# Reordering the output product of a hybrid RWKV-7 / short-convolution layer on one core

## The chip, the cores and the metric

The kernel runs on one core of one Trainium2 chip. The metric is the device time of one execution in microseconds (us), of which a smaller number is better. Every time in this part is from the runs of the kernel before or from the trace of one profiled execution of it.

## The reference

One layer takes 512 tokens, with 16 learned tokens put before them, each 2048 wide.

```python
hn = rmsnorm(h_res, norm_in_g)
P = hn @ w_in                              # 2048 -> 65 column groups of 128
r, k, v, g_r, wl, al = token_shift(P[:, :4224])    # RWKV-7 branch, 16 heads x 64
Bg, Cg, hc, g_c = split(P[:, 4224:])               # convolution branch, 1024 wide
y_a = (group_norm(recurrence(r, decay, k, v, kk, kk * a)) + bonus) * silu(g_r)
y_b = Bg * causal_conv3(Cg * hc, conv_w) * silu(g_c)
mix = concat([y_a, y_b])                   # 2048 wide
h_res = h_res + mix @ w_out                # 2048 x 2048
out = rmsnorm(h_res, norm_f_g)[16:]
```

All values are float32.

## The kernel before

**Stages.** The input projection (`mains`, `steps`) makes 65 column groups of 128 with TensorE. The RWKV branch is worked out beside it in four rounds of two head pairs: `prepare` makes the operands of one pair, `invert` inverts the triangular systems of two pairs, and `recur` then runs the recurrence over nine chunks. When the projection's last group (`ps_gc`) is done, the output product follows, with the final RMS norm at its end. On TensorE the order is the program's own. The other engines' instructions, SyncE's DMA queue among them, are put in order by a scheduler, except for the last stretch of the kernel, whose order is written out by hand.

**Precision.** Every large matmul is done three times, as high x high, high x low and low x high parts. The high part of a tensor is a copy that ScalarE rounds (CAST), the low part is a subtraction on VectorE of two operands (TENSOR_TENSOR). A "split" below is this pair of instructions.

**The work between matmuls.** `fill(ns)` puts that much projection work (in the program's own estimate) into TensorE's order, so that another engine has time for the next step of `prepare`, `invert` or `recur`. The table `FW` holds the amounts. In `invert`, `fill(FW["solve_first"])` stands ahead of the first use of the inverse: VectorE's transposes `xn` (L844) and then TensorE's `t` (L853).

**The output product.** `mix @ w_out` is done for two halves of 1024 output columns. In each half the operands are cut into 2 x 2 quarters and multiplied by seven products in place of eight (a Strassen-Winograd scheme): `M1`, `M2`, `P5`, `M7`, `M3`, `Q6`, `P4`. The left operands are parts of `mix` (for M1, M2, P4) or four sums of such parts, the forms `S1`, `S3`, `S4`, `S5`, each made for two quarters of mix rows, q = 0 and 1 (`sums` on VectorE, then `split_form`; tiles named `S` in the trace). The right operands are blocks of `w_out` (128 x 1024), or sums of such blocks.

A product of one half is cut in four parts g = 0 to 3 along the inner dimension. One `(half, product, g)` is a **unit**, called a block here: twelve matmuls of 512 columns. The list `units` is the order of the 56 blocks on TensorE. In the kernel before it is, for each half, M1 (4 blocks), then for each g the four blocks P5, M7, M3, Q6, then P4 and M2: mixed with each other in the first half, P4 ahead of M2 in the second. The half-1 M2 blocks are not in that loop: they end the kernel (`end`, `ends`).

**Weights of a block.** Three kinds of buffers are used.

- `raw` is a ring of three buffers, which the projection's weights (`wr`) use before and `request` uses here (tiles `wo`).
- `chain` is one tile per g (`x` in the trace). `begin_chain` loads it on SyncE's queue, `add_by_transfer` adds another block to it by an accumulating DMA on GpSimd's queue, `add` adds one on VectorE (L1204). P5, Q6 and P4, and M1 with another content, take their weights from it. In half 0 the tiles 0 to 2 are loaded while the projection still runs; tile 3 lies in a pool (`pw`) that opens when the projection's buffers are given up.
- The split parts go to a ring of six slots (`w` of the projection, `o` here), two for a block, so a block's slots come free when the block three places ahead is done. The half-1 M2 weights are split early into buffers of their own (`load_home`).

`at(u, fn, ...)` puts a step in front of block u. After the four blocks of a product, `close` adds its result to the output tiles `xa` (columns 0 to 1023) or `xb` (1024 to 2047) on VectorE (`onto`, L1222) and takes squares on ScalarE. `gain` multiplies finished tiles by the norm's weights `gfb`; eight of these run on GpSimd (L1299). At the end `row_scale` makes the RMS factor of a token tile, with a power on GpSimd (`rsqrt`, L98), and `finish` and `finish_last` scale the output and store it.

```python
    for half in range(2):
        units += [(half, "M1", g) for g in range(4)]
        units += [(half, prod, g) for g in range(4) for prod in ("P5", "M7", "M3", "Q6")]
        ends = ("P4", 0), ("P4", 1), ("M2", 0), ("P4", 2), ("M2", 1), ("P4", 3), ("M2", 2), ("M2", 3)
        units += [(half, prod, g) for prod, g in sorted(ends, key=lambda e: half and e[0] == "M2")]
```

Of the kernel before, what the change touches and what calls it, by code (L numbers as in the profile page):

```python
# [9 lines left out]
F32 = mybir.dt.float32  # L10
# [3 lines left out]
ALU = mybir.AluOpType  # L14
# [4 lines left out]
P = 128  # L19
# [58 lines left out]
def hymba_kernel(ctx: ExitStack, tc: tile.TileContext, xt, xtok, front, w_in, w_out, pv, lup, cst, msk, gf, out):  # L78
    nc = tc.nc
# [3 lines left out]
    wp = ctx.enter_context(tc.tile_pool(name="wp", bufs=3))  # L83
# [105 lines left out]
    raw = {}  # L189
# [920 lines left out]
    def quarter(k, tk, q):  # L1110
        return mix[2 * k + q][:, :, tk]

    def sums(q):
        a11, a21, a12, a22 = quarter(0, T0, q), quarter(0, T1, q), quarter(1, T0, q), quarter(1, T1, q)
        nc.vector.tensor_tensor(out=a22, in0=a22, in1=a21, op=ALU.subtract)
        nc.vector.tensor_tensor(out=a21, in0=a11, in1=a21, op=ALU.subtract)
        nc.vector.scalar_tensor_tensor(out=a11, in0=a22, scalar=-1.0, in1=a11, op0=ALU.mult, op1=ALU.subtract)
        nc.vector.scalar_tensor_tensor(out=a12, in0=a11, scalar=-1.0, in1=a12, op0=ALU.mult, op1=ALU.subtract)

    for j in range(NPAIR, NPAIR + 4):  # L1120
        split_mix(j)
# [13 lines left out]
    for j in range(NPAIR + 4, KT):  # L1135
        while ("gc", j - NPAIR) not in ready:
            step()
        run_pending(float("inf"))
        split_mix(j)
    for _ in flow:  # L1140
        pass
    prefetch(len(stream))
    ph1.close()


# [16 lines left out]


    LEFT = {"M1": 0, "M2": T0, "M7": "S3", "Q6": "S5", "P5": "S1", "P4": T1, "M3": "S4"}
    units = []
    for half in range(2):
        units += [(half, "M1", g) for g in range(4)]
        units += [(half, prod, g) for g in range(4) for prod in ("P5", "M7", "M3", "Q6")]
        ends = ("P4", 0), ("P4", 1), ("M2", 0), ("P4", 2), ("M2", 1), ("P4", 3), ("M2", 2), ("M2", 3)
        units += [(half, prod, g) for prod, g in sorted(ends, key=lambda e: half and e[0] == "M2")]  # L1170
    U = {unit: u for u, unit in enumerate(units)}
    right, straight = {}, {}

    def left(prod, jj, part, s):
        w = LEFT[prod]
# [4 lines left out]
            return parts[jj][part][:, tk]  # L1180
        return parts[NPAIR + jj][part][:, w][:, tk]

    def rows_of(half, k, col, g):
        return w_out[2 * half + col, 4 * k + g]

    def begin_chain(half, g):
        if half or g == 3:
            chain[g] = new_chain(half, g)  # L1190
        nc.sync.dma_start(chain[g], rows_of(half, 0, 0, g))

    def request(half, k, col, g):
        t = wp.tile([P, 1024], F32, tag="raw", name=f"wo{half}{k}{col}{g}", bufs=3)
        state["dma"] = nc.sync.dma_start(t, rows_of(half, k, col, g)).ins
        straight[half, k, col, g] = t
# [83 lines left out]
    def at(u, fn, *args):  # L1280
        calls.setdefault(max(u, -1), []).append((fn, args))
# [31 lines left out]
    def passing(*block):  # L1313
        return lambda: straight[block]

    def chained(g):
        return lambda: chain[g]

    for half in range(2):
        o = 28 * half  # L1320
        for g in range(4):
            b = o + 4 + 4 * g
            if half == 0:
                if g == 3:
                    at(-1, begin_chain, 0, g)
                    at(0, split_unit, (0, "M1", g), chained(g))
            else:
                at(o + g - 4, begin_chain, 1, g)
                at(o + g - 2, split_unit, (1, "M1", g), chained(g))
            at(max(o + g, b - 5), add_by_transfer, half, 0, 1, g)  # L1330
# [10 lines left out]
            if half == 0:  # L1341
# [79 lines left out]
    with tc.manual_schedule(engines={mybir.EngineType.DVE, mybir.EngineType.Activation, mybir.EngineType.Pool}):  # L1421
        end = po.tile([P, 512], F32, tag="o", name="end")
        for g in range(4):
            product((1, "M2", g), [end], (0,))
        for t in (2, 3):
            row_part(t, 3)
            row_scale(t, 3)
        row_part(0, 3)
        row_part(1, 3)
        finish(2, (2, 0, 3))  # L1430
        finish(3, (2,))
        nc.vector.tensor_tensor(out=here(0, 2), in0=here(0, 2), in1=end, op=ALU.add)
        squares(0, 2)
        row_scale(0, 3)
        finish(3, (0, 3))
        gain(1, 3, nc.vector)
        ends = [po.tile([P, 256], F32, tag="o", name=f"end{part}") for part in range(2)]
        for part in range(2):
            cols = slice(256 * part, 256 * part + 256)
            for jj in range(8):  # L1440
                hi, lo = right[(1, "M2", jj // 2), jj % 2]
                for n, (m, w) in enumerate(((0, hi), (0, lo), (1, hi))):
                    nc.tensor.matmul(
                        ends[part], left("M2", jj, m, 1), w[:, cols], start=(jj == 0 and n == 0), stop=(jj == 7 and n == 2)
                    )
            h = here(1, 2)[:, cols]
            nc.vector.tensor_tensor(out=h, in0=h, in1=ends[part], op=ALU.add)
# [70 lines left out]
```

## Time and profile before

| what | value |
|---|---|
| median of 3 runs | 1012.8 us (1012.61 to 1014.0) |
| time of the profiled execution | 1012.36 us |
| its span, first to last instruction | 1010.6 us |
| TensorE (PE) busy | 995.3 us, 98% |
| VectorE (DVE) busy | 684.2 us, 68% |
| ScalarE (ACT) busy | 393.8 us, 39% |
| GpSimd (POOL) busy | 276.8 us, 27% |
| granted TensorE clock, mean | 0.998 |
| last matmul of the projection, first of the output product | 842.09 us, 842.31 us |

Times in the trace count from the start of the span. A row of the timeline has the start, the length, the engine, the line, the operation, the tiles (output <- inputs), the shape and how many like instructions follow each other; in brackets stands how long the engine was idle before the row, and what ended that. The ends of matmuls are modelled and matmuls overlap, so a wait of TensorE is read best from the starts of rows: with no wait a block of twelve matmuls takes a fixed time.

### The profile page before, as it was taken

Reading aid. Unit: us, or ns where it says so; the run is one execution under the profiler, and the core shown is the slowest. Engines: PE = TensorE matmul, PEld = TensorE weight load, DVE = VectorE, ACT = ScalarE, POOL = GpSimd, SP = SyncE. Lnnn points to the kernel's source line nnn. Section 1 sums busy time; section 2 is a strip of 40 time slices with the busy share of each in tenths; the row PEclk is TensorE's granted clock in tenths of the full one; section 3 lists DMA queues with packets and bytes.
Section 4 is the critical chain, followed back from the end, with each engine's and each line's share of the span. In section 5 each row is a group of like instructions: output and inputs, shape, how many; then the busy total and the mean of one; then the engine's idle time right before and its main releaser. Section 6 shows DMA issues by size and latency. Waiting matters only on the chain.

```text
span 1010.6 us, 23763 instructions
## 1 busy us (share of the span) xinstructions
PE 995.3 (98%) x9723; PEld 913.0 (90%) x9723; DVE 684.2 (68%) x1305; ACT 393.8 (39%) x729; POOL 276.8 (27%) x294
## 2 busy tenths in 40 slices
PE   9999999999999999999999999999999999999996
PEld 8999998999998999998999998889898897787875
DVE  7686955588765668654668653254555697998787
ACT  7553423344323434322434322222222335445453
POOL 0123314233232423232324222222333332015001
PEclk9999999999999999999999999999999999999999
DMA  9526476346764363854273856977772798695654
GB/s 331 156 73 151 121 203 171 108 124 152 173 162 145 93 170 98 221 148 120 84 187 92 211 140 207 339 244 228 217 213 76 212 262 192 168 325 140 173 122 167
DMA packets 185037, 174.83 MB, mean 173 GB/s; under 512 B 121568, under 2 KB 142816, under 8 KB 184416
## 3 DMA queue, kind: packets, MB, share of 16 engines
q1 hardware_dynamic: 182336, 164.40, 56.5%
q0 software_dynamic: 2304, 8.39, 5.0%
q8 instruction: 76, 1.25, 0.5%
q10 hardware_dynamic: 288, 0.52, 0.1%
q14 instruction: 33, 0.27, 0.1%
HBM read 136.92 MB, written 36.35 MB: 171 GB/s over the span
## 4 chain that ended last, share of the span: by engine, by line
PE 56%; DVE 8%; DMA 3%; issue 2%; ACT 1%; POOL 0%; DVEq 0%; ACTq 0%; SPq 0%; POOLq 0%
PE ps_gc L328 8%; PE ps_B L328 7%; PE ps_h L328 7%; PE ps_C L328 7%; PE ps_k L328 5%; PE ps_v L328 5%; PE ps_g L328 5%; PE ps_r L328 5%; DVE o L1214 3%; DMA wo<-in_w_out_dram 2%; PE M L1241 2%; PE zy L1010 1%; PE zs L1006 1%; PE g L681 1%; DVE xb L1222 1%
## 5 line engine op out<-in xcount | busy, mean ns | idle before, releaser
L135 POOL TENSOR_TENSOR w<-wr,w 128x512 fp32r<-128x512 f32 x119 | 167.5, 1408 | 358.2 <-ACT w L134 307.4
L134 ACT CAST w<-wr 128x512 fp32r<-128x512 f32 x252 | 153.2, 618 | 286.4 <-PE ps_k L328 46.8
L135 DVE TENSOR_TENSOR w<-wr,w 128x512 fp32r<-128x512 f32 x133 | 96.1, 729 | 102.2 <-ACT w L134 102.0
L328 PE MATMUL ps_r<-xh,w 128*128 128x256 f32 (+1 forms) x512 | 95.5, 282 | 0.0
L328 PE MATMUL ps_k<-xh,w 128*128 128x256 f32 (+1 forms) x512 | 95.5, 284 | 0.0
L328 PE MATMUL ps_v<-xh,w 128*128 128x272 f32 (+1 forms) x512 | 95.1, 283 | 0.0
L328 PE MATMUL ps_h<-xh,w 128*128 128x258 f32 (+1 forms) x512 | 94.0, 282 | 0.7 <-issue 0.7
L328 PE MATMUL ps_C<-xh,w 128*128 128x258 f32 (+1 forms) x512 | 93.2, 281 | 0.0
L328 PE MATMUL ps_g<-xh,w 128*128 128x258 f32 (+1 forms) x512 | 92.2, 281 | 0.0
L328 PE MATMUL ps_B<-xh,w 128*128 128x512 f32 x256 | 83.6, 395 | 0.1
L328 PE MATMUL ps_gc<-xh,w 128*128 128x512 f32 x256 | 81.5, 393 | 0.2 <-DVE w L135 0.2
L328 PEld LDWEIGHTS ps_h<-xh,w 128*128 128x128 f32 x512 | 79.7, 189 | 1.5 <-issue 0.8
L328 PEld LDWEIGHTS ps_k<-xh,w 128*128 128x128 f32 x512 | 80.4, 189 | 0.2
L328 PEld LDWEIGHTS ps_r<-xh,w 128*128 128x128 f32 x512 | 80.4, 189 | 0.2
L328 PEld LDWEIGHTS ps_v<-xh,w 128*128 128x128 f32 x512 | 80.1, 189 | 0.3
L328 PEld LDWEIGHTS ps_C<-xh,w 128*128 128x128 f32 x512 | 79.7, 189 | 0.6
L328 PEld LDWEIGHTS ps_g<-xh,w 128*128 128x128 f32 x512 | 79.4, 189 | 0.5
L328 PE MATMUL ps_k<-xl,w 128*128 128x272 f32 (+1 forms) x256 | 73.0, 285 | 0.0
L328 PE MATMUL ps_v<-xl,w 128*128 128x256 f32 (+1 forms) x256 | 72.5, 283 | 0.0
L328 PE MATMUL ps_r<-xl,w 128*128 128x256 f32 (+1 forms) x256 | 72.3, 282 | 0.0
L328 PE MATMUL ps_g<-xl,w 128*128 128x256 f32 (+1 forms) x256 | 72.2, 282 | 0.0
L328 PE MATMUL ps_C<-xl,w 128*128 128x256 f32 (+1 forms) x256 | 71.9, 281 | 0.0
(321 smaller groups left out, 2275.6 us busy)
## 6 DMA issues: line engine op xcount, KB each, us to landing
wr<-in_w_in_dram SPq DMA_DIRECT2D x126, 512.0 KB
ct<-opd SPq DMA_DIRECT2D x64, 288.0 KB
wo<-in_w_out_dram SPq DMA_DIRECT2D x24, 512.0 KB
x<-in_w_out_dram POOLq DMA_DIRECT2D x16, 512.0 KB, 5.8
opd<-ar SPq DMA_DIRECT2D x8, 576.0 KB
opd<-gt SPq DMA_DIRECT2D x16, 288.0 KB
opd<-bt SPq DMA_DIRECT2D x64, 64.0 KB
x<-in_w_out_dram SPq DMA_DIRECT2D x8, 512.0 KB
```

Of the source, the lines that this page charges most:

```text
L134: nc.scalar.copy(hi, rq)
L135: low[q] = eng.tensor_tensor(out=lo, in0=rq, in1=hi.bitcast(F32), op=ALU.subtract).ins
L328: nc.tensor.matmul(ps[r], ww[:, w], xx[:, kt, a:b], start=(kt == 0 and n == 0), stop=(kt == KT - 1 and n == 2))
L681: nc.tensor.matmul(z[h][:, c - c0], bk[hs, c, h : h + 2, :].rearrange("p a s -> p (a s)"), ar[hs, c].rearrange("p a s -> p (a s)"), start= ...
L1006: nc.tensor.matmul(d[hs, j], w, x[hs], start=(a == 0), stop=(a == b - 1))
L1010: nc.tensor.matmul(d[ho, j], t[hs, o : o + CH], x[hs], start=(a == 0), stop=(a == b - 1))
L1214: nc.vector.tensor_tensor(out=lo, in0=rq, in1=hi.bitcast(F32), op=ALU.subtract)
L1222: nc.vector.tensor_tensor(out=h, in0=h, in1=ps, op=op)
L1241: nc.tensor.matmul(bank[s], left(prod, jj, m, s), w, start=(jj == 0 and n == 0), stop=(jj == 7 and n == 2))
```

## The change

- **Order of the blocks.** In half 0 the four M2 blocks stand right behind the four M1 blocks and ahead of the first P5. The P4 blocks of half 0 end that half, and the first M1 block of half 1 stands ahead of the last P4 block. Half 1 keeps its order. The steps that load and split weights move with their blocks.
- **Weights of the fourth M1 block of half 0** come through a `raw` buffer, requested while the projection still runs, instead of through chain tile 3. That tile is loaded later, at block 2.
- **Forms.** The four sums of `sums(1)` are spread over blocks 6 to 9, and the eight `split_form` steps over blocks 1 to 14.
- **First inverse.** `FW["solve_first"]` gets 1100 more, so more projection work stands ahead of the first inverse's matmuls.
- **End.** The last `gain` of the token tile 1 (256 columns, VectorE) stands behind `row_scale` instead of ahead of it, and one `finish` of token tile 0 behind the last addition instead of ahead of it.

```diff
-        fill(FW["solve"] + 2400 * (first == 2) if first else FW["solve_first"])
+        fill(FW["solve"] + 2400 * (first == 2) if first else FW["solve_first"] + 1100)
...
     prefetch(len(stream))
+    straight = {}
+    request(0, 0, 0, 3)
     ph1.close()
...
+    def block(half):
+        return [(half, prod, g) for g in range(4) for prod in ("P5", "M7", "M3", "Q6")]
+
+    units = [(0, prod, g) for prod in ("M1", "M2") for g in range(4)] + block(0)
+    units += [(0, "P4", 0), (0, "P4", 1), (0, "P4", 2), (1, "M1", 0), (0, "P4", 3)]
+    units += [(1, "M1", g) for g in range(1, 4)] + block(1) + [(1, prod, g) for prod in ("P4", "M2") for g in range(4)]
...
+    at(0, split_unit, (0, "M1", 3), passing(0, 0, 0, 3))
+    at(2, begin_chain, 0, 3)
...
-            if half == 0:
-                at(U[half, "M2", g] - 4, request, 0, 1, 0, g)
-                at(U[half, "M2", g] - 2, split_unit, (0, "M2", g), passing(0, 1, 0, g))
+            if half:
+                at(m2 + 2 * g - g - 11, load_home, g)
             else:
-                at(o + 13 + 2 * g, load_home, g)
+                at(m2 - 5, request, 0, 1, 0, g)
+                at(m2 - 2, split_unit, (0, "M2", g), passing(0, 1, 0, g))
     for n, f in enumerate(("S1", "S3", "S4", "S5")):
-        at(n, split_form, f, 0)
-        if n == 2:
-            at(n + 1, sums, 1)
-        at(6 + n, split_form, f, 1)
+        at((1, 2, 4, 5)[n], split_form, f, 0)
+        at(6 + n, sums, 1, (n,))
+        at((10, 11, 13, 14)[n], split_form, f, 1)
...
-            gain(1, 2, nc.vector, cols)
             if part == 0:
-                finish(0, (2, 0, 3))
+                gain(1, 2, nc.vector, cols)
+                finish(0, (2, 0))
                 nc.vector.tensor_tensor(out=fv[:, 1, 0:1], in0=fv[:, 1, 0:1], in1=ssq[:, 1, 3:4], op=ALU.add)
+        finish(0, (3,))
         row_scale(1, 4, nc.vector)
+        gain(1, 2, nc.vector, slice(256, 512))
         finish_last(1)
```

Three places of the engines' orders are shown, as the built programs have them, before and after. A row has the line, the operation, output <- inputs with buffer numbers, and the shape.

VectorE, from the last projection split of `mix` on, before (`x_11314` is chain tile 3, `x_11136` chain tile 0, `wo` raw buffers, `o` slots, `S` forms):

```order
L1105 TENSOR_TENSOR m_11274<-mix_10660,m_11273 128x512
L1115 TENSOR_TENSOR mix_10660<-mix_10660,mix_10658 128x4x256
L1161 TENSOR_TENSOR S_11295<-mix_10659,S_11294 128x1024
L1161 TENSOR_TENSOR S_11291<-mix_10657,S_11290 128x1024
L1214 TENSOR_TENSOR o_0_11317<-x_11314,o_0_11317 128x512
L1214 TENSOR_TENSOR o_1_11320<-x_11314,o_1_11320 128x512
L1214 TENSOR_TENSOR o_0_11355<-x_11136,o_0_11355 128x512
L1214 TENSOR_TENSOR o_1_11358<-x_11136,o_1_11358 128x512
L1161 TENSOR_TENSOR S_11297<-mix_10659,S_11296 128x1024
L1214 TENSOR_TENSOR o_0_11378<-wo_11310,o_0_11378 128x512
```

The same place after (the splits' line is L1216, the forms' L1174):

```order
L1105 TENSOR_TENSOR m_11274<-mix_10660,m_11273 128x512
L1216 TENSOR_TENSOR o_0_11314<-wo_11277,o_0_11314 128x512
L1216 TENSOR_TENSOR o_1_11317<-wo_11277,o_1_11317 128x512
L1118 TENSOR_TENSOR mix_10660<-mix_10660,mix_10658 128x4x256
L1174 TENSOR_TENSOR S_11297<-mix_10659,S_11296 128x1024
L1216 TENSOR_TENSOR o_0_11356<-wo_11312,o_0_11356 128x512
L1216 TENSOR_TENSOR o_1_11359<-wo_11312,o_1_11359 128x512
L1174 TENSOR_TENSOR S_11293<-mix_10657,S_11292 128x1024
L1174 TENSOR_TENSOR S_11299<-mix_10659,S_11298 128x1024
L1216 TENSOR_TENSOR o_0_11383<-wo_11320,o_0_11383 128x512
```

The fourth M1 block's split (the first two `o` rows of each) is now first and reads a raw buffer, and M2 splits (`wo_11312`, `wo_11320`) stand where those of P5 and M7 stood.

GpSimd, from the chain additions of the end of half 0 on, before (DMA rows are chain additions, the others are gains):

```order
L1200 DMA x_11138<-in_w_out_dram 128x1024
L1200 DMA x_11314<-in_w_out_dram 128x1024
L1299 TENSOR_TENSOR xa_11308<-xa_11308,gfb 128x512
L1299 TENSOR_TENSOR xa_11306<-xa_11306,gfb 128x512
L1299 TENSOR_TENSOR xa_11309<-xa_11309,gfb 128x512
L1299 TENSOR_TENSOR xa_11307<-xa_11307,gfb 128x512
L1299 TENSOR_TENSOR xa_11308<-xa_11308,gfb 128x512
L1200 DMA x_11860<-in_w_out_dram 128x1024
L1299 TENSOR_TENSOR xa_11309<-xa_11309,gfb 128x512
L1200 DMA x_11880<-in_w_out_dram 128x1024
```

The same place after:

```order
L1301 TENSOR_TENSOR xa_11308<-xa_11308,gfb 128x512
L1301 TENSOR_TENSOR xa_11309<-xa_11309,gfb 128x512
L1202 DMA x_11138<-in_w_out_dram 128x1024
L1202 DMA x_11354<-in_w_out_dram 128x1024
L1202 DMA x_11826<-in_w_out_dram 128x1024
L1301 TENSOR_TENSOR xa_11310<-xa_11310,gfb 128x512
L1301 TENSOR_TENSOR xa_11308<-xa_11308,gfb 128x512
L1301 TENSOR_TENSOR xa_11311<-xa_11311,gfb 128x512
L1202 DMA x_11872<-in_w_out_dram 128x1024
L1301 TENSOR_TENSOR xa_11309<-xa_11309,gfb 128x512
```

Two gains moved ahead of the chain additions for P4's last blocks (`x_11138`, `x_11354`), and the first chain addition of half 1 (`x_11826`) moved ahead of the other six gains. The first of those six needs the result of P4.

VectorE at the very end, before (`end` is the result of the last products, L1393 and L1299 are `row_scale` and `gain`):

```order
L1403 SCALAR_TENSOR_TENSOR xb_11802<-xb_11802,fv,gfb 128x512
L1452 TENSOR_TENSOR fv<-fv,ssq 128x1
L1447 TENSOR_TENSOR xb_11780<-xb_11780,end_12546 128x256
L1299 TENSOR_TENSOR xb_11780<-xb_11780,gfb 128x256
L1393 TENSOR_SCALAR fv<-ssq,fv 128x1
```

The same place after:

```order
L1450 TENSOR_TENSOR fv<-fv,ssq 128x1
L1445 TENSOR_TENSOR xb_11781<-xb_11781,end_12548 128x256
L1401 SCALAR_TENSOR_TENSOR xb_11806<-xb_11806,fv,gfb 128x512
L1391 TENSOR_SCALAR fv<-ssq,fv 128x1
L1301 TENSOR_TENSOR xb_11781<-xb_11781,gfb 128x256
```

The finish (L1401) moved behind the last addition, and the gain (L1301) behind `row_scale` (L1391).

More of the change, by code (lines that the diff above doesn't have):

```diff
@@ L1111, in quarter, with sums @@
         return mix[2 * k + q][:, :, tk]
-    def sums(q):
+    def sums(q, which=range(4)):
         a11, a21, a12, a22 = quarter(0, T0, q), quarter(0, T1, q), quarter(1, T0, q), quarter(1, T1, q)
[L1115 to L1118, printed above, removed]
+        for n in which:
+            if n < 2:
+                o, x = ((a22, a22), (a21, a11))[n]
+                nc.vector.tensor_tensor(out=o, in0=x, in1=a21, op=ALU.subtract)
+            else:
+                o, x = ((a11, a22), (a12, a11))[n - 2]
+                nc.vector.scalar_tensor_tensor(out=o, in0=x, scalar=-1.0, in1=o, op0=ALU.mult, op1=ALU.subtract)
     for j in range(NPAIR, NPAIR + 4):
@@ L1139, in hymba_kernel, with rows_of, request @@
         split_mix(j)
+    def rows_of(half, k, col, g):
+        return w_out[2 * half + col, 4 * k + g]
+    def request(half, k, col, g):
+        t = wp.tile([P, 1024], F32, tag="raw", name=f"wo{half}{k}{col}{g}", bufs=3)
+        state["dma"] = nc.sync.dma_start(t, rows_of(half, k, col, g)).ins
+        straight[half, k, col, g] = t
     for _ in flow:
@@ L1164, in hymba_kernel @@
     LEFT = {"M1": 0, "M2": T0, "M7": "S3", "Q6": "S5", "P5": "S1", "P4": T1, "M3": "S4"}
[L1165 to L1170, printed above, removed]
+    def block(half):
[3 more added lines that the diff above has]
+    units += [(1, "M1", g) for g in range(1, 4)] + block(1) + [(1, prod, g) for prod in ("P4", "M2") for g in range(4)]
     U = {unit: u for u, unit in enumerate(units)}
-    right, straight = {}, {}
+    right = {}
     def left(prod, jj, part, s):
@@ L1191, in begin_chain @@
         nc.sync.dma_start(chain[g], rows_of(half, 0, 0, g))
[L1193 to L1196, printed above, removed]
     def add_by_transfer(half, k, col, g):
@@ L1317, in chained @@
         return lambda: chain[g]
+    at(0, split_unit, (0, "M1", 3), passing(0, 0, 0, 3))
+    at(2, begin_chain, 0, 3)
     for half in range(2):
-        o = 28 * half
         for g in range(4):
-            b = o + 4 + 4 * g
-            if half == 0:
[L1324 to L1330, printed above, removed]
+            b, m1, m2 = U[half, "P5", g], U[half, "M1", g], U[half, "M2", g]
+            if half:
+                at(m1 - 4, begin_chain, 1, g)
+                at(m1 - 2, split_unit, (1, "M1", g), chained(g))
+            at(max(m1 + (half == 0 and g == 3), b - 5), add_by_transfer, half, 0, 1, g)
             at(b - (6 if g else 5), request, half, 0, 1, g)
```

4 lines of the change are left out of this document (1 added, 3 removed).

## Prediction

> **What bounds the kernel now.** I read the page first, then TensorE's timeline over the output product, then VectorE, ScalarE and GpSimd over the same stretch, and last the projection as one window.
>
> ```profile
> span 1010.6 us, 23763 instructions
> PE 995.3 (98%) x9723; PEld 913.0 (90%) x9723; DVE 684.2 (68%) x1305; ACT 393.8 (39%) x729; POOL 276.8 (27%) x294
> 178.00:842.30 664.30, 663.52 (x7576) 620.50 (x7569) 413.99 (x829) 223.91 (x414) 206.15 (x198) 1.00 0.62 171
> ```
>
> TensorE is busy for 98% of the span, and the change removes no matmul. What can be won is time in which TensorE stands, and the row of the window (length, then busy time of PE, PEld, DVE, ACT and POOL) says that between the first inverse and the end of the projection it stands for 0.8 us of 664. So the output product is what to look at:
>
> ```profile
> 842.31 8.33 PE L1241 MATMUL M<-w,m 128*128 128x512 f32 x36
> 851.52 0.51 PE L1241 MATMUL M<-o,m 128*128 128x512 f32 x1 [0.88 <-ACT o L1213]
> 854.90 2.89 PE L1241 MATMUL P<-o,S 128*128 128x512 f32 x12
> 862.14 2.14 PE L1241 MATMUL M<-o,S 128*128 128x512 f32 x8 [0.71 <-DVE o L1214]
> 865.07 2.80 PE L1241 MATMUL Q<-o,S 128*128 128x512 f32 x11 [0.57 <-DVE o L1214]
> 878.95 2.88 PE L1241 MATMUL P<-o,S 128*128 128x512 f32 x12
> 917.02 9.55 PE L1241 MATMUL M<-o,m 128*128 128x512 f32 x40
> 926.81 3.01 PE L1241 MATMUL M<-o,m 128*128 128x512 f32 x12 [0.24 <-DVE o L1214]
> 930.16 4.84 PE L1241 MATMUL M<-o,m 128*128 128x512 f32 x20 [0.34 <-DVE o L1214]
> 934.85 2.88 PE L1241 MATMUL P<-o,S 128*128 128x512 f32 x12
> 970.21 5.94 PE L1241 MATMUL M<-o,S 128*128 128x512 f32 x24
> 990.71 0.61 PE L1241 MATMUL end<-home,m 128*128 128x512 f32 x2
> ```
>
> Fourteen blocks lie between 878.95 and 917.02, with no wait in them: 38.07 us, 2.719 us a block. By this measure TensorE loses 12.59 - 4 x 2.719 = 1.71 us from 842.31 to 854.90, 24.05 - 8 x 2.719 = 2.30 us up to 878.95, 17.83 - 6 x 2.719 = 1.52 us from 917.02 to 934.85, nothing over the 13 blocks after that, and 20.50 - 7 x 2.719 = 1.47 us from 970.21 to 990.71. Together 7.0 us: all that a better order of blocks can give.
>
> **Why it waits.** Four rows for the first two losses:
>
> ```profile
> 845.46 0.33 SPq L1191 DMA_DIRECT2D x<-in_w_out_dram  x1
> 850.85 2.18 ACT L1213 CAST o<-x 128x512 fp32r<-128x512 f32 x4 [1.95 <-DMA x<-in_w_out_dram]
> 864.34 2.49 DVE L1214 TENSOR_TENSOR o<-x,o 128x512 fp32r<-128x512 f32 x4
> 855.00:875.00 20.00, 20.00 (x26) 1.00 0.59 139
> ```
>
> The fourth M1 block's weights are asked for at 845.46, when the projection's buffers come free, and land at about 850.8, after the block could have begun (842.31 + 3 x 2.719 = 850.47). Then VectorE is busy for 20.00 of 20.00 us: eight forms, four sums and the weights of P5 to Q6 all fall due within it. A split takes 0.60 us there (four in 2.49, with a tail of 0.08), a 1024-wide sum or form 1.14. For the third loss:
>
> ```profile
> 902.76 1.28 DVE L1266 TENSOR_TENSOR sh<-sh,Q 128x512 f32<-128x512 f32 x2
> 907.61 4.69 DVE L1222 TENSOR_TENSOR xa<-xa,sh 128x512 f32<-128x512 f32 x4
> 909.75 1.39 POOL L1299 TENSOR_TENSOR xa<-xa,gfb 128x512 f32<-128x512 f32 x1 [0.30 <-ACT sqj_None L1228]
> 925.38 1.38 DVE L1214 TENSOR_TENSOR o<-x,o 128x512 fp32r<-128x512 f32 x1 [0.76 <-ACT o L1213]
> 928.72 5.17 DVE L1214 TENSOR_TENSOR o<-x,o 128x512 fp32r<-128x512 f32 x5 [0.16 <-ACT o L1213]
> 842.50:936.30 93.80, 87.50 (x113) 1.00 0.75 208
> ```
>
> Two VectorE instructions take 1.28 us beside no GpSimd work; four with both operands in SBUF take 4.69 us beside GpSimd's gains, and single splits 1.38. So a gain costs VectorE up to 1.1 us. TensorE's waits at 926.81 and 930.16 end just behind such splits.
>
> **The change, part by part.** *M2 behind M1, the fourth M1 block from a raw buffer.* The raw buffer's request stands ahead of the chains in SyncE's queue, during the projection, so its weights lie ready; the 1.71 us go. M2 needs no form and no sum, only splits, so P5 of g = 0 begins at block 8, not 4: 842.31 + 8 x 2.719 = 864.06 where nothing waits. I counted VectorE's new order against this, from 846.8 (the end of the last split of `mix`, which stays) at 0.60 and 1.14 us a row. The second M7 split of g = 1 is done at 877.2, against 842.31 + 13 x 2.719 + 0.68 = 878.3, the tightest place of this part; P5 of g = 0 at 862.0 against 864.7. The raw ring's requests pass too: M2's third weights are asked for when M1's fourth are split (848.0), and even 5.4 us (asked 845.46, cast 850.85) leave them over 4 us ahead of block 6. So I take all of the 2.30 us too.
>
> *P4 late, M1 of half 1 among it.* Chain tile 0 of half 1 is asked for behind P4's first split and is due at block 27 (915.7); VectorE's count brings both there early. What decides is VectorE's total. From 842.5 to the end of M7's first split in half 1 (936.3) it was busy 87.5 of 93.8 us, 6.3 idle. In the new order the same stretch holds one 1024-wide addition more, which earlier ran under the projection: 88.6 us. That split is due at 842.31 + 33 x 2.719 + 0.68 = 932.7, which leaves it 1.6 us of idling in place of 6.3. Since a block's slots come free only three blocks later, it can't run far ahead and will stand when it has caught up, by my count some 3 us around blocks 20 to 23. That makes it about 1.4 us late. The two ends: 0 if it idles under 1.6 us, 4.7 if it idles as much as before. I take 1.4, since VectorE's count has it two to three us ahead of most blocks, which is work done in time that was idle. GpSimd's six gains behind P4 fall into just these blocks, where they were spread over 907 to 933 before. So of 1.71 + 2.30 + 1.52 = 5.53 us I expect 4.1.
>
> *The end of half 1.* The order there is the same but for buffers, and VectorE's lead on TensorE about the same: 0, between 0.45 gained (VectorE half a us earlier in its chain of weight requests) and 1.0 lost.
>
> *First inverse.*
>
> ```profile
> 170.04 2.37 DVE L135 TENSOR_TENSOR w<-wr,w 128x512 fp32r<-128x512 f32 x2
> 172.34 0.70 DVE L844 STREAM_TRANSPOSE xn<-xT 128x512 f32<-128x512 f32 x1
> 173.09 0.69 PE L853 MATMUL t<-xn,gt 64*64 64x64 f32 x32 [0.79 <-DVE xn L844]
> ```
>
> Ten projection matmuls of 272 columns, 10 x 0.12 = 1.2 us by the same pace, now stand ahead of these. The 0.79 us go, and the transpose does not move on VectorE. I take 0.8 off.
>
> *The end of the kernel.*
>
> ```profile
> 996.14 5.91 PE L1443 MATMUL end<-home,m 128*128 128x256 f32 x48
> 1001.24 1.41 DVE L1403 SCALAR_TENSOR_TENSOR xb<-xb,fv,gfb 128x512 f32<-128x512 f32 x2
> 1002.63 0.41 DVE L1447 TENSOR_TENSOR xb<-xb,end 128x256 f32<-128x256 f32 x1
> 1003.68 0.42 DVE L1299 TENSOR_TENSOR xb<-xb,gfb 128x256 f32<-128x256 f32 x1 [0.64 <-ACT sqj L1228]
> 1004.02 0.21 DVE L1393 TENSOR_SCALAR fv<-ssq,fv 128x1 f32<-128x1 f32 x1
> 1004.31 0.55 POOL L98 TENSOR_TENSOR fv<-fv,mhalf 128x1 f32<-128x1 f32 x1 [3.62 <-DVE fv L1393]
> 995.89 0.30 POOL L1393 TENSOR_SCALAR fv<-ssq,fv 128x1 f32<-128x1 f32 x1
> 999.52 0.52 POOL L1393 TENSOR_SCALAR fv<-ssq,fv 128x1 f32<-128x1 f32 x1 [2.40 <-ACT sqj_None L1228]
> ```
>
> TensorE is done at 1002.05; the last addition (1002.63) waits for two finishes on VectorE. With one moved behind it, it starts about 0.5 us sooner, and the finish runs under ScalarE's squares. With the gain moved behind `row_scale`, that row comes a further 0.34 us sooner (1004.02 - 1003.68): 0.8 together. But the gain then runs beside GpSimd's power. A GpSimd row of the same form took 0.30 us alone and 0.52 beside a gain, so I give 0.3 of it back and take 0.5 (0.3 to 0.8). The Trainium skill (SBUF — State Buffer, "SBUF: two separate sides") says that VectorE with two SBUF inputs and GpSimd share one port pair that is locked for a whole instruction. By that the power waits for the rest of the gain; the trace's 1.38 us splits agree, and this term is then 0.5, without the lock 0.8.
>
> **The sum.** 4.1 + 0 + 0.8 + 0.5 = 5.4 us off the profiled execution's 1012.36, which is 0.44 under the median: 1007.0, or **1007.4** on the median's scale. The likely case's own range is 1006.0 to 1009.4.
>
> **Rivals.**
>
> *All waits go.* VectorE idles little, and its gains meet idle time: 5.53 + 0.45 + 0.8 + 0.8 = 7.6 us off, 1005.2. For it speaks that one of the gains before (at 919.60) fell into VectorE's idle time; against it, that 88.6 of 90.2 us must then be work. Chance 0.20.
>
> *VectorE is what sets the pace.* It idles as much as before, since slots and chains hold it, and the end of half 1 starts late: 4.7 us come back there and 1.0 at the end. 5.53 - 4.7 - 1.0 + 0.8 + 0.3 = 0.9 us off, 1011.9, no measurable change. For it: 20.00 busy of 20.00. Against: VectorE has M2's 10.9 us more before the forms fall due. Chance 0.13, of which 0.08 end within 0.2%.
>
> *Slower: the weights of the low-rank step come late in the projection.* The later inverse re-lays VectorE's order for some 40 us. The split `lul` of the next head pair moves from ahead of `te` to behind the transpose `vs`:
>
> ```profile
> 203.71 0.96 DVE L595 TENSOR_TENSOR lul<-lur,luh 128x256 fp32r<-128x256 f32 x1 [0.47 <-ACT luh L594]
> 216.55 0.78 DVE L821 STREAM_TRANSPOSE vs<-v 128x576 f32<-128x576 f32 x1
> 230.14 0.29 PE L572 MATMUL tz<-la,lul 128*128 128x272 f32 x1
> ```
>
> It would be done at about 218, 12 us ahead of its matmul. Held up for longer than that, TensorE, in its fixed order, stands for every us beyond, and it has no slack in the projection. 20 us of delay cost 8: 1012.36 + 8 - 5.4 = 1015.0, 1015.4 on the median's scale. It is slower from 12 + 5.4 us on. Against it: 12 us of lead. Chance 0.07.
>
> The forecast keeps 0.60. The range takes in all the first rival and most of the second: 1004.4 to 1011.0. Faster by over 0.2% (2.0 us, about what a measurement here can tell from no change): 0.60 + 0.20 + 0.05 = 0.85; within it 0.08; slower 0.07.
>
> **What would show it.** Right: the first P block starts 22 us behind the first output matmul, with no wait of TensorE in the eight blocks ahead; no wait at L853 near 173; the first P block of half 1 starts 88 to 89 us behind the first output matmul (92.5 before), with gains on GpSimd and VectorE rows of 1.3 us and more right there. The sum is wrong if TensorE waits anew between 175 and 842, if M2's blocks wait for a DMA, or if the first P block of half 1 starts under 87.3 us or over 91 us behind the first.

## The result, and the profile after

| | kernel before | changed kernel |
|---|---|---|
| median of 11 runs of each | 1013.52 us (1012.36 to 1014.97) | 1010.73 us (1008.48 to 1013.13) |
| ratio of the two, 95% interval | 1 | 0.9973 [0.9964, 0.9983] |
| profiled execution | 1012.36 us | 1008.48 us |

The changed kernel is 2.7 us faster (0.27%), where 5.4 us were forecast. Both profiled executions are the fastest of their eleven, and the changed kernel's times spread over 4.7 us where those of the kernel before spread over 2.6. So one trace does not tell all of this result, and the experiments below give twelve more traces.

The page of the changed kernel, first lines of the part on engines:

```profile
span 1006.6 us, 23759 instructions
PE 993.2 (99%) x9723; PEld 912.7 (91%) x9723; DVE 683.2 (68%) x1305; ACT 393.0 (39%) x729; POOL 288.0 (29%) x294
```

TensorE's timeline over the output product, with the places that answer to those shown of before:

```profile
842.02 8.33 PE L1243 MATMUL M<-w,m 128*128 128x512 f32 x36
850.19 13.76 PE L1243 MATMUL M<-o,m 128*128 128x512 f32 x60
863.79 2.88 PE L1243 MATMUL P<-o,S 128*128 128x512 f32 x12
907.31 8.32 PE L1243 MATMUL P<-o,m 128*128 128x512 f32 x36
929.07 2.92 PE L1243 MATMUL P<-o,S 128*128 128x512 f32 x12
931.83 0.39 PE L1243 MATMUL M<-o,S 128*128 128x512 f32 x1
933.16 5.55 PE L1243 MATMUL M<-o,S 128*128 128x512 f32 x23 [0.95 <-DVE o L1216]
939.28 2.77 PE L1243 MATMUL Q<-o,S 128*128 128x512 f32 x11 [0.35 <-DVE o L1216]
969.67 2.82 PE L1243 MATMUL M<-o,S 128*128 128x512 f32 x11 [0.19 <-DVE o L1216]
981.68 5.51 PE L1243 MATMUL P<-o,m 128*128 128x512 f32 x23 [0.28 <-DVE o L1216]
987.03 5.15 PE L1243 MATMUL end<-home,m 128*128 128x512 f32 x22
```

The first P block starts 863.79 - 842.02 = 21.77 us behind the first output matmul, just what eight blocks take, and TensorE does not wait until 931.83. The waits at the start of the output product are gone. From 931.83 on it waits for VectorE's splits: in the second and the fourth block behind the M1 blocks of half 1 (numbers 33 and 35, counted from 0), and again near the end. The 52 blocks take 987.03 - 842.02 = 145.01 us, of which 145.01 - 52 x 2.719 = 3.6 us are waits (7.0 before).

What VectorE and GpSimd do just ahead of that first wait (rows of each engine in turn):

```profile
914.28 7.21 POOL L1301 TENSOR_TENSOR xa<-xa,gfb 128x512 f32<-128x512 f32 x1 [1.02 <-ACT sqj_None L1230]
925.47 1.59 POOL L1301 TENSOR_TENSOR xa<-xa,gfb 128x512 f32<-128x512 f32 x1
927.32 1.90 POOL L1301 TENSOR_TENSOR xa<-xa,gfb 128x512 f32<-128x512 f32 x1
929.18 2.23 POOL L1301 TENSOR_TENSOR xa<-xa,gfb 128x512 f32<-128x512 f32 x1
914.30 2.50 DVE L1224 TENSOR_TENSOR xa<-xa,sh 128x512 f32<-128x512 f32 x4
917.91 1.22 DVE L1206 TENSOR_TENSOR wo<-wo,wo 128x1024 f32<-128x1024 f32 x1
919.05 1.29 DVE L1216 TENSOR_TENSOR o<-x,o 128x512 fp32r<-128x512 f32 x2
920.25 0.69 DVE L1224 TENSOR_TENSOR xa<-xa,P 128x512 f32<-128x512 f32 x1
925.38 4.45 DVE L1216 TENSOR_TENSOR o<-x,o 128x512 fp32r<-128x512 f32 x1
929.86 2.64 DVE L1206 TENSOR_TENSOR x<-x,wo 128x1024 f32<-128x1024 f32 x1
```

A gain begins at 914.28 and lasts 7.21 us, while VectorE runs one instruction with two SBUF operands behind the other; it ends just behind the first VectorE row with a PSUM operand (920.25). Then it is GpSimd that keeps VectorE out: one split (two take 1.29 us at 919.05) lasts 4.45 us and ends only behind two gains and the two chain additions issued among them, and the 1024-wide addition behind it takes 2.64 us in place of 1.22. TensorE's wait at 931.83 is for the splits that stand behind these two rows.

### The profile page after: what moved, and what is told of

Same layout as the page of the kernel before. It is cut to its first block, busy times and chain, and to the rows that moved or that the text cites. A ratio compares the mean times of both kernels' runs of the same rounds, so it can differ in the third digit from the quotient of the medians.

```text
span 1006.6 us, 23759 instructions
## 1 busy us (share of the span) xinstructions
PE 993.2 (99%) x9723; PEld 912.7 (91%) x9723; DVE 683.2 (68%) x1305; ACT 393.0 (39%) x729; POOL 288.0 (29%) x294
## 4 chain that ended last, share of the span: by engine, by line
PE 62%; DVE 5%; DMA 2%; issue 2%; ACT 0%; POOL 0%; DVEq 0%; ACTq 0%; POOLq 0%
PE ps_gc L328 8%; PE ps_B L328 7%; PE ps_h L328 7%; PE ps_C L328 7%; PE ps_k L328 5%; PE ps_v L328 5%; PE M L1243 5%; PE ps_g L328 5%; PE ps_r L328 5%; DVE o L1216 2%; PE P L1243 2%; DMA wo<-in_w_out_dram 2%; PE Q L1243 1%; PE zy L1010 1%; PE zs L1006 1%
```

## The experiments

A table of all traces first. Kernels of one group of runs share the runs of the kernel before, so ratios compare better than medians. "Start" is the first output matmul. The next four columns are what TensorE loses in the output product against 2.719 us a block, worked out from the starts of its rows: in blocks 0 to 7, 8 to 26, 27 to 35 and 36 to 51. "End" is the time from the end of block 51 to the end of the span. All in us.

| kernel | median (runs) | ratio to before, 95% | start | 0-7 | 8-26 | 27-35 | 36-51 | end |
|---|---|---|---|---|---|---|---|---|
| before | 1013.5 (11) | 1 | 842.31 | 3.64 | 0.38 | 1.51 | 1.48 | 19.89 |
| changed | 1010.73 (11) | 0.9973 [0.9964, 0.9983] | 842.02 | 0.02 | 0.02 | 1.95 | 1.63 | 19.53 |
| a1, changed again | 1009.36 (5) | 0.9965 [0.9952, 0.9977] | 842.39 | 0.02 | 0.02 | 1.36 | 2.75 | 19.43 |
| a2, changed again | 1008.24 (1) | - | 842.13 | 0.02 | 0.02 | 1.42 | 1.95 | 19.40 |
| no_gain | 1006.36 (5) | 0.9924 [0.9911, 0.9938] | 842.53 | 0.02 | 0.02 | 0.01 | 0.54 | 19.47 |
| g_dve2 | 1007.74 (5) | 0.9943 [0.9930, 0.9955] | 842.76 | 0.02 | 0.02 | 0.01 | 2.04 | 19.59 |
| g_dve3 | 1005.76 (5) | 0.9926 [0.9913, 0.9939] | 842.38 | 0.02 | 1.47 | 0.01 | 0.49 | 19.17 |
| g_dve4 | 1005.51 (5) | 0.9920 [0.9907, 0.9934] | 841.82 | 0.02 | 0.02 | 0.01 | 0.15 | 19.19 |
| g_pool2 | 1009.17 (5) | 0.9961 [0.9947, 0.9975] | 842.08 | 0.02 | 0.02 | 1.45 | 2.46 | 19.45 |
| c3late | 1009.19 (5) | 0.9954 [0.9941, 0.9966] | 842.29 | 0.02 | 0.02 | 1.37 | 2.41 | 19.61 |
| no_inv | 1010.16 (5) | 0.9967 [0.9954, 0.9979] | 843.08 | 0.02 | 1.28 | 2.48 | 2.12 | 19.21 |
| tail0 | 1010.51 (7) | 0.9976 [0.9965, 0.9987] | 842.26 | 0.02 | 0.88 | 2.43 | 1.90 | 19.83 |
| b_ng, old order | 1011.24 (11) | 0.9978 [0.9969, 0.9987] | 843.88 | 4.37 | 0.37 | 0.01 | 0.02 | 19.80 |
| raw, old order | 1011.92 (11) | 0.9990 [0.9981, 0.9999] | 843.40 | 2.27 | 0.38 | 1.27 | 1.37 | 19.88 |

**The changed kernel again (a1, and later a2).**

> The changed kernel as it is, for a second trace and for the spread of its times (1008.5 to 1013.1 so far, where the kernel before had 1012.4 to 1015.0). Theory P (a GpSimd gain and a VectorE instruction with two SBUF inputs shut each other out, so that the start of half 1 depends on how they fall): a time in the middle of the spread goes with TensorE waits of 2 to 5 us at blocks 27 to 36, where the first trace shows 1.8 us, and the rest of the trace agrees within 0.5 us. Rival Q (the spread comes from waits that the change does not touch, such as those of the projection near 760 and at the kernel's start): the blocks 27 to 36 lose 1.8 us again, and the difference of the spans lies ahead of 842.

> The changed kernel as it is, for a third trace. Five traces have the same output product and the same GpSimd gains (the changed kernel twice, without the later inverse, with the old end, and with VectorE gains as a contrast). If its time is set by two things that fall differently each time, the landing of M2's last weights near 857 (VectorE waited 0.5 us for it in one trace, 2.3 and 2.5 in others) and how the gains and VectorE meet from 915 on, then the time from the first output matmul to the end of P4 of half 1 lies between 145.0 and 147.3 us, and the share over 141.4 (52 blocks of 2.719) splits into a part in blocks 8 to 27 of the size of VectorE's wait near 857 less 1 us, and the rest behind block 27.

Both theories of a1 were partly right. The losses behind block 26 are 3.6, 4.1 and 3.4 us in the three traces of the same program; in a1 and a2 the first of the late gains got through in 1.77 us, and the waits fell in blocks 30 and 31 instead of 33 and 35. The starts differ by 0.4 us as well. Neither trace is from the slow end of the spread (1012 to 1013), so what such an execution loses was not seen. From the first output matmul to the end of P4 of half 1 a2 takes 144.8 us, just under the 145.0 to 147.3 that were expected. The split of its expectation holds: VectorE does not wait near 857, nothing is lost in blocks 8 to 26, and the rest lies behind.

**Without six gains (no_gain), and with them on VectorE (g_dve2).**

```diff
-    for n in range(8):
+    for n in (0, 2):
         at(30 + 2 * n, gain, n // 2, n % 2, nc.gpsimd)
+    for m, n in enumerate((1, 3, 4, 5, 6, 7)):      # g_dve2 alone; issued behind the last split
+        at(38 + m + m // 2, late_gain, n // 2, n % 2)
```

`late_gain` is here a gain on VectorE, issued behind the last split made so far.

> The changed kernel without the six GpSimd gains behind P4 (the output lacks that factor in six 128x512 blocks). Theory P: TensorE loses under 0.4 us in blocks 27 to 36 in place of 1.8, the time falls by 1.5 to 3 us against the changed kernel, and its spread shrinks to under 2.5 us. Rival V (VectorE's total work sets the pace there, gains or not): blocks 27 to 36 still lose over 1.2 us and the time falls by under 0.7 us. Rival Q: the spread stays at 4 us and more.

> The changed kernel with these six gains on VectorE, one each among blocks 40 to 46 (0.60 us each, 3.6 us in all, where VectorE idles 8.4 of 27 us), so that no GpSimd gain runs beside VectorE's splits of half 1. Theory P: blocks 27 to 36 lose under 0.4 us, blocks 46 to 51 at most 0.6 us more than the 1.4 us of the first trace; 1 to 2.5 us under the changed kernel. Rival V: no gain, within 0.7 us of the changed kernel, or up to 2 us slower through blocks 46 to 51.

TensorE in the trace without the gains, start of half 1 and the only wait that is left:

```profile
929.58 2.88 PE L1243 MATMUL P<-o,S 128*128 128x512 f32 x12
932.30 5.60 PE L1243 MATMUL M<-o,S 128*128 128x512 f32 x24
937.74 2.88 PE L1243 MATMUL Q<-o,S 128*128 128x512 f32 x12
979.14 5.52 PE L1243 MATMUL P<-o,m 128*128 128x512 f32 x23 [0.15 <-DVE o L1216]
```

The six gains are what TensorE waits for at the start of half 1: without them blocks 27 to 35 lose nothing, and 3.0 us of the 3.6 are gone. VectorE's total work (rival V) does not make these waits. Nor do the chain additions, which stay on GpSimd: beside one (923.89 to 924.78) two splits take 1.37 us (924.32). The five times lie within 1.7 us, against 2.9 in a1 and 4.7 before that, as theory P has it; but no_inv, with its gains, has 1.5 too, so five runs are few for that.

The losses in blocks 36 to 51 mostly go too, though no gain runs there. VectorE does not carry work over to them: in blocks 36 to 46 it idles 8.4 us with the gains and 8.2 without, most of it until weights (`wo`) land. These are asked for as the ring's buffers come free, and the first request behind the late splits leaves 91.7 us behind the first output matmul with the gains (933.74), 85.9 without (928.43). Behind the last of these waits VectorE never idles up to the end of block 51. Its first row there, with the gains and then without:

```profile
967.72 1.29 DVE L1216 TENSOR_TENSOR home<-wo,home 128x512 fp32r<-128x512 f32 x2 [2.57 <-ACT home L1215]
```

```profile
965.18 1.29 DVE L1216 TENSOR_TENSOR home<-wo,home 128x512 fp32r<-128x512 f32 x2 [2.41 <-ACT home L1215]
```

The two start 125.70 and 122.65 us behind the first output matmul, 3.05 us apart. TensorE is 1.94 us later by then, and the difference, 1.1 us, is what it loses more in blocks 36 to 51 (1.63 against 0.54). The same sum fits nine more traces (before, a1, a2, g_dve3, g_dve4, c3late, no_inv, tail0, raw) to 0.03 us.

With the gains on VectorE in blocks 38 to 47, blocks 27 to 35 are free of waits as well, but part of the 3.6 us of added work, ahead of and inside that last stretch, comes back as one wait:

```profile
974.88 5.72 PE L1243 MATMUL P<-o,m 128*128 128x512 f32 x24 [1.17 <-DVE o L1216]
```

**Gains on VectorE, earlier (g_dve3), and later on GpSimd (g_pool2).** The first is g_dve2 with `at` at blocks 33, 35, 36, 37, 39 and 40. The second leaves them on GpSimd, behind chain additions:

```diff
+    def late_gain(t, n):
+        with tc.issue_after(state["pool"]):
+            gain(t, n, nc.gpsimd)
...
+        at(35 + m + 2 * (m // 2), late_gain, n // 2, n % 2)
```

> The changed kernel with the six gains on VectorE, one each among blocks 34 to 41, some five blocks earlier than in the run before, where VectorE idled 9 us in the trace without gains (922 to 954). Theory P, with VectorE saturated from 970 on: the wait of 1.3 us at 973 shrinks to under 0.5 us, blocks 27 to 36 lose under 0.5 us, and the time is 0.7 to 1.3 us under the kernel with the later VectorE gains, some 0.5 us above the one without gains. Rival V: a VectorE debt of 3.6 us comes back wherever the gains stand; within 0.4 us of the later placement.

> The changed kernel with the six gains still on GpSimd, but two each behind the chain additions near 940, 950 and 960. If the place alone mattered (a crowded VectorE stretch), this is as good as the six on VectorE: 1 to 2.5 us under the changed kernel. If the engine matters (theory P: each gain costs VectorE up to 1.1 us more than the 0.6 us that it costs when VectorE does it), blocks 27 to 36 lose under 0.5 us but VectorE starts the stretch from 970 late, TensorE waits 2 us or more at 965 to 985, and the time is 0.5 to 1.5 us above that of the six on VectorE.

The earlier place brings the loss in blocks 36 to 51 from 2.04 to 0.49 us, and by the ratios the time falls by another 1.7 us, where 0.7 to 1.3 were expected (the two intervals overlap, but the slowest of the five times lies under the fastest of g_dve2's): VectorE idles there, and the work costs nothing. Its trace lost 1.47 us elsewhere, in blocks 8 to 26 (below). The GpSimd variant did not do what was meant: its rows show four of the six gains behind chain additions at 921 and 926, not at 940 and 950.

```profile
920.71 0.86 POOL L1202 DMA_DIRECT2D x<-in_w_out_dram  x1 [1.47 <-DVE o L1216]
921.28 2.86 POOL L1301 TENSOR_TENSOR xa<-xa,gfb 128x512 f32<-128x512 f32 x2
926.92 2.85 POOL L1301 TENSOR_TENSOR xa<-xa,gfb 128x512 f32<-128x512 f32 x2
960.67 2.85 POOL L1301 TENSOR_TENSOR xa<-xa,gfb 128x512 f32<-128x512 f32 x2
960.81 3.88 DVE L1216 TENSOR_TENSOR o<-x,o 128x512 fp32r<-128x512 f32 x2
```

So as a whole it does not tell place from engine. The two gains at 960 do stand where VectorE had just idled 3.2 us, and beside them two splits take 3.88 us in place of 1.29. Waits of TensorE follow, of 0.7 us at 963 and 0.5 us at 973; the second has its like in the changed kernel (969.67).

**The old order without the gains (b_ng).** The same line of the kernel before, `for n in (0, 2)`.

> The kernel before without six of its eight GpSimd gains (the output lacks that factor in six 128x512 blocks). Theory P (the gains cost VectorE, and through it TensorE, in the old order too): the 1.5 us that blocks 28 to 30 lose go, and the time falls by 1.5 to 2.5 us against the kernel before. Then the two orders without gains stand 5 us apart (4.0 of the first two losses, 0.6 of the inverse, 0.4 of the end). Rival V (the old order of VectorE's work made these waits): they stay, the time falls by under 0.7 us, and without gains the orders stand 7 us apart.

The losses in blocks 27 to 51 go from 2.99 to 0.03 us, so the old order paid for the gains as well, and the 1.48 us at its end were theirs too. The time falls by 2.2 us (1.3 to 3.1), as theory P has it. Without gains the orders stand 0.9978 - 0.9924 = 0.0054 apart, 5.5 us, close to the 5.0 expected.

**One part alone: the raw buffer in the old order (raw).** The fourth M1 block's weights come by `request(0, 0, 0, 3)` during the projection, all else as before.

> The kernel before with one part of the change alone: the fourth M1 block's weights through a raw buffer, asked for while the projection runs. If its wait was worth 1.7 us by itself, the first P5 block starts 4 x 2.719 = 10.9 us behind the first output matmul in place of 12.6 and the time falls by 1.7 us. If VectorE's eight forms and four sums right behind it are the bound (rival), the blocks P5 to Q6 wait so much longer, the ninth block still starts 25 us and more behind the first, and the time falls by under 0.7 us.

```profile
843.40 8.33 PE L1243 MATMUL M<-w,m 128*128 128x512 f32 x36
854.29 2.88 PE L1243 MATMUL P<-o,S 128*128 128x512 f32 x12
861.82 2.14 PE L1243 MATMUL M<-o,S 128*128 128x512 f32 x8 [0.78 <-DVE o L1216]
864.76 2.83 PE L1243 MATMUL Q<-o,S 128*128 128x512 f32 x11 [0.56 <-DVE o L1216]
```

The first P block starts 10.89 us behind the first matmul, and the output product is 1.7 us shorter than in the trace of before. The second loss stays as it was (2.27 and 0.38 us), so the two losses are separate, and the rival falls by the trace (the ninth block starts 24.0 us behind the first, not 25). The times gained 1.0 us (0.1 to 1.9), less than the 1.7 expected, and by themselves they would not tell the two apart. The new place of M2 and of the forms has no run of its own: its part is read from the traces, where blocks 0 to 7 lose 0.02 us in all eleven of the new order, and blocks 8 to 26 as little in eight of them.

**The inverse and the end undone (no_inv, tail0).** Without `+ 1100`; and with the whole `gain` and three finishes ahead of `row_scale`, as before.

> The changed kernel with the first inverse where it was before (without the 1100). If the inverse's term is right, TensorE waits 0.7 to 1.0 us again at the first t, near 172, and the output product starts about 0.8 us later in the span; time 0.8 us above the changed kernel. If the later inverse only moves the wait to another place of the projection (rival), the wait at t comes back and the output product starts within 0.3 us of where it does in the changed kernel's traces.

> The changed kernel with the end as it was before (all of the last gain ahead of row_scale, three finishes of token tile 0 ahead of the last addition). If the end's term of the prediction (0.5 us) is right, the stretch from the last P4 block to the end of the span is 19.9 us again, where the four traces of kernels with the changed end had 19.4 to 19.6 us; time 0.3 to 0.5 us above the changed kernel, which the times alone may not tell. Rival (the end waits for something else): 19.5 us as with the change.

```profile
173.27 0.69 PE L853 MATMUL t<-xn,gt 64*64 64x64 f32 x32 [0.79 <-DVE xn L844]
```

The wait at `t` comes back with its old length. By the ratios alone (0.9967 and 0.9976 against 0.9965 and 0.9973) neither part could be told from nothing. The start of the output product moves from one trace to the next even with the same projection, by 0.9 us among the ten traces with the later inverse and by 1.6 us among the four without. So means are needed: 842.27 and 843.17, 0.9 us apart, of which four such traces make a rough figure. The end takes 19.85 us in the four traces with the old code and 19.41 in the ten with the new one, 0.44 us. VectorE's rows at the end, with the change and then undone:

```profile
998.42 0.42 DVE L1445 TENSOR_TENSOR xb<-xb,end 128x256 f32<-128x256 f32 x1
999.47 0.21 DVE L1391 TENSOR_SCALAR fv<-ssq,fv 128x1 f32<-128x1 f32 x1
999.76 0.66 POOL L98 TENSOR_TENSOR fv<-fv,mhalf 128x1 f32<-128x1 f32 x1 [2.73 <-DVE fv L1391]
```

```profile
1000.80 0.41 DVE L1445 TENSOR_TENSOR xb<-xb,end 128x256 f32<-128x256 f32 x1
1002.19 0.21 DVE L1391 TENSOR_SCALAR fv<-ssq,fv 128x1 f32<-128x1 f32 x1
1002.48 0.55 POOL L98 TENSOR_TENSOR fv<-fv,mhalf 128x1 f32<-128x1 f32 x1 [3.62 <-DVE fv L1391]
```

`row_scale` follows the addition by 1.05 us in place of 1.39, and the power beside the gain takes 0.11 us longer.

**Late weights (c3late, g_dve4).** Three traces lose 0.9 to 1.5 us in blocks 8 to 26, where none of the gains behind P4 has begun. SyncE's queue, ScalarE and VectorE in one of them (no_inv), at M2's last weights (asked for with the first of the three requests):

```profile
852.26 5.01 SPq L1148 DMA_DIRECT2D wo<-in_w_out_dram  x3
859.70 1.14 ACT L1215 CAST o<-wo 128x512 fp32r<-128x512 f32 x2 [2.99 <-DMA wo<-in_w_out_dram]
860.35 0.69 DVE L1216 TENSOR_TENSOR o<-wo,o 128x512 fp32r<-128x512 f32 x1 [2.31 <-ACT o L1215]
```

VectorE idles 2.3 us there, 2.5 in g_dve3 and 1.7 in tail0 (there in two main waits, 0.86 us ahead of 855.75 and 0.75 ahead of 863.85); TensorE loses 1.28, 1.47 and 0.88 us. In the other eight traces of the new order VectorE idles 0 to 0.5 us and TensorE loses nothing. So the reserve is about 1 us (2.31 - 1.28, 2.49 - 1.47 and 1.71 - 0.88 us), and what is beyond it is lost. c3late moves the load of chain tile 3 behind later weight requests; g_dve4 is g_dve3 with that. (`behind` issues a transfer behind the last weight request made so far.)

```diff
-        nc.sync.dma_start(chain[g], rows_of(half, 0, 0, g))
+        if half:
+            nc.sync.dma_start(chain[g], rows_of(half, 0, 0, g))
+        else:
+            behind(chain[g], rows_of(half, 0, 0, g))
...
-    at(2, begin_chain, 0, 3)
+    at(8, begin_chain, 0, 3)
```

> The changed kernel with the load of chain tile 3 of half 0 behind the weight requests of blocks 8 and on, not ahead of M2's third and fourth. Theory L (transfers ahead in the queue make M2's last weights land late, and VectorE, saturated from 858 on, hands the delay to TensorE): ACT casts M2's fourth weights by about 856, VectorE waits under 0.3 us there, blocks 8 to 27 lose under 0.2 us, and the slow end of the times falls by 0.5 to 1 us; median 0 to 1 us under the changed kernel. Rival (the landing is late for another reason, such as the loads of xa): VectorE still waits 0.5 us or more at 857, times as before.

> The gains on VectorE in blocks 34 to 41 and the late load of chain tile 3 together. The trace of the first alone lost 1.45 us in blocks 8 to 27 behind a VectorE wait of 2.5 us at 857. Theory L: that goes, from first output matmul to the end of P4 of half 1 it takes 141.8 to 142.3 us, and the median is 0.5 to 1.2 us under the kernel with the VectorE gains alone (1005.8). Rival: within 0.4 us of it.

Both traces have no such idling, but neither have six of the other nine of this order, and the medians differ by less than the runs of one kernel do (1009.19 against 1009.36, 1005.51 against 1005.76). So theory L is not shown, and by the times g_dve4 goes with its rival (within 0.4 us): that the late load helps is not settled. The trace of g_dve4 has an output product with next to no wait at all (window: length, then busy time of PE, PEld, DVE, ACT and POOL):

```profile
841.82:983.40 141.58, 141.58 (x625) 117.04 (x624) 131.91 (x186) 77.83 (x137) 20.59 (x16) 1.00 0.72 192
```

The same window of the changed kernel is 3.4 us longer with the same VectorE time, though VectorE has six instructions fewer there:

```profile
842.02:987.03 145.01, 143.18 (x626) 116.58 (x625) 131.78 (x180) 77.34 (x137) 35.61 (x22) 1.00 0.70 187
```

g_dve4 beats both kernels: 0.9920 [0.9907, 0.9934] of the time before, 8 us.

## Why the prediction was right or wrong

**The direction and most of the places were right.** M1 and M2 run without a wait, the first P block starts at 21.77 us (22 forecast), the wait at `t` is gone, and the gains meet VectorE at the start of half 1, as forecast. But the first P block of half 1 starts 929.07 - 842.02 = 87.05 us behind the first output matmul in the profiled execution, under the 87.3 that the prediction named as a sign of a wrong sum: nothing is lost up to there, and the waits come one block later. In a1 and a2 it starts at 88.3, inside the 88 to 89 forecast.

**The first step that failed: "What decides is VectorE's total" (1.4 us given back) and "the end of half 1: 0".** The 1.4 us were VectorE's idle time: some 3 us around blocks 20 to 23, less the 1.6 that it could spare. With the 1.47 us at the end, taken to stay, that makes 2.9 us of waits behind block 26. They measure 3.4 to 4.1 us in the three traces of the changed kernel, and 4.6 and 4.3 in no_inv and tail0, which have the same output product. It is luck that 1.4 lies near the 1.4 to 2.0 us that these three lose in blocks 27 to 35. In the new order VectorE idles at most 0.1 us in blocks 20 to 23, and its total does not decide: without the six gains the waits behind block 26 are 0.5 us, and in g_dve4, where VectorE does the gains as well, 0.2. What decides these waits is that the gains and VectorE's two-operand instructions shut each other out, for 7.21 us on the one side and 4.45 on the other in the profiled trace. The prediction saw that the gains would fall there, and priced one at up to 1.1 us of VectorE, but its sum has no term of their own for them. And the 1.47 us at the end was no part of the order that stays: without gains it is 0.5 us in the new order and nothing in the old.

**The second: "I take all of the 2.30 us too".** The raw ring's requests were said to leave M2's third weights 4 us ahead of their block, with 5.4 us from the request to the cast. The fourth took 859.70 - 852.26 = 7.4 us in no_inv. TensorE did not wait for them, but VectorE did, and VectorE's own reserve is about 1 us. In three of eleven traces of the new order that gave back 0.9 to 1.5 us. The prediction did call the M7 split of g = 1 the tightest place, and there (block 13) these three traces lose 0.45 us.

**The inverse (0.8) and the end (0.5)** measure 0.9 and 0.44 us. At the end the wait goes as worked out, and part of the give-back is the power's 0.11 us. By the Trainium skill (SBUF — State Buffer, "SBUF: two separate sides") GpSimd and VectorE with two SBUF inputs share one port pair, which the one that starts first holds for its whole instruction. The trace agrees that the gains and the splits exclude each other (4.45 us for a split of 0.69). The sum drew on its own rows at the end; the lock-out mattered in the middle of the kernel.

**The scale.** Of the profiled pair the sum gives 1007.0 for a measured 1008.48. The 0.44 us from the trace to the median was taken from three runs; over eleven it is 1.16 us, and for the changed kernel 2.25 us, whose profiled execution was its fastest. The trace of before began its output product at 842.31, the other three without the later inverse at 843.08 to 843.88, so the pair of traces shows only 0.29 us of the inverse's 0.8.

**What stays open.** The gains took about 1.1 us more than forecast (4.0 against 2.9, mean of five traces), late weights 0.3 us on the mean of eleven traces. That turns the 5.4 us into about 4.0. The first eleven runs show 2.7 us (1.7 to 3.6), the five of a1 3.5 (2.3 to 4.9). What the slower executions of the changed kernel lose beyond this is in no trace.

**The rivals.** "All waits go" (1005.2) is not what the changed kernel does. g_dve4 comes to it (1005.5) with the gains moved, although it was VectorE's 88.6 us of work in 90.2 that the prediction held against it. "VectorE sets the pace" was right about the last stretch of half 1 only, where VectorE never idles. The late split `lul` cost nothing; the waits of TensorE between 178 and 842 have one row (in total, times, longest), and what it names is no other engine:

```profile
PE zy L1010 <- issue: 1.3, 1, 1.3
```

## What to carry to other kernels

- Work that is given to GpSimd because it is idle is not free when VectorE is full of instructions with two SBUF operands: price it at the length of the run that it meets, not at its own length, or give it to VectorE where that engine idles. Here six multiplications of 128x512 cost TensorE 3 us on GpSimd in blocks 26 to 32, and next to nothing on VectorE in blocks 33 to 40.
- When a change fills the engine that feeds TensorE, count its reserve, not TensorE's: weights that are in time for the matmul can be late for the split.
- Take the price of a term from several traces if the times spread by more than the term.

## What the runs showed of the hardware

- A GpSimd multiplication of two SBUF operands that takes 1.29 us at its shortest took 7.64 and 7.21 us in the changed kernel's trace. Past the second of these went nine VectorE instructions with two SBUF operands, between 914.3 and 920.3, and the next gain started at 921.46. By the Trainium skill (SBUF — State Buffer, "SBUF: two separate sides") the one that starts first holds the shared port pair for its whole instruction, and the other blocks. The trace agrees that they exclude each other, but here the gain waited for a whole row of instructions, until one came with a PSUM operand; the 7.64 us ended in a gap of VectorE (890.42 to 891.92). The ends of GpSimd's rows are rough, but VectorE's 4.45 us and TensorE's wait behind it are not.

```profile
L1301 POOL TENSOR_TENSOR xa<-xa,gfb x8: 1288/1827/7639, 883.9 to 929.2; 128x512 f32<-128x512 f32 x8
```

- The same program met itself differently each time: the first late gain lasted 7.21, 1.77 and 1.77 us in three traces, and the place of TensorE's waits moved with it (blocks 33 and 35, or 30 and 31).
